# A chunked delta rule: ScalarE's and VectorE's steps put in another order, another bank for an output transpose, and an inversion's 64x64 products paired

## The chip, the cores and the metric

The kernel runs on one core of a Trainium2 chip. The metric is device time in microseconds (us) of one execution: 2244.25 us is the median of three runs before the change (2241.93 to 2248.31). The engines are TensorE (PE; PEld is its weight load), VectorE (DVE), ScalarE (ACT), GpSimd (POOL) and SyncE (SP, which issues most DMAs).

## The reference

A two-layer encoder step over 2048 prompt tokens and 32 sample tokens, width 1024, float32. Layer one is a gated delta rule with 8 heads of 128; layer two is sliding-window attention. What matters here is the delta rule. It is evaluated in blocks of positions; within a block a unit lower triangular matrix has to be inverted (or solved with), and a 128x128 state `s` per head goes from block to block:

```python
lower = jnp.where(strict, jnp.einsum('nbhik,nbhjk->nbhij', kbeta, kc) * decay, 0.0)
tmat = lower + jnp.eye(c, dtype=lower.dtype)
u = lax.linalg.triangular_solve(tmat, vc * bc[..., None], left_side=True, lower=True, unit_diagonal=True)
...
def step(s, xs):
    qd, kd, ui, wi, ai, gl = xs
    v_new = ui - jnp.einsum('bhck,bhkv->bhcv', wi, s)
    o = jnp.einsum('bhck,bhkv->bhcv', qd, s) + jnp.einsum('bhij,bhjv->bhiv', ai, v_new)
    s = s * gl[..., None, None] + jnp.einsum('bhck,bhcv->bhkv', kd, v_new)
    return s, o
```

## The kernel before

The kernel goes through stages: projections of q, k, v with a short convolution (class `P1`, up to about 720 us of the profiled execution), the delta rule with what is left of the gate projection as filler (class `Delta`, about 720 to 1190 us), output products and layer norm (`O1`), the second layer's projections (`P2`) and attention. The change touches only the delta stage.

The delta stage has 17 chunks: one of the 32 sample tokens and 16 of 128 prompt tokens. `Delta.run` is one loop over them, written as generators that are advanced by hand: `go(a, b, ...)` takes one step of each, and the order of these calls is the order in which instructions are put on PE, DVE and ACT (each works its own list in that order). One turn of the loop works on several chunks at once: state products of chunk `ch`, inversion of the next (`nx`), keys, values and triangular matrix of the one after (`n2`), decays of the third (`n3`). The steps by name:

- `lower` (n2): products k k^T into bank `g`, times the decays `E` on DVE into `npr`; ACT copies the diagonal 32x32 blocks to `nb`, DVE transposes them to `L`. `chain` inverts these blocks column by column, 25 columns on POOL, the last six on DVE a turn later. `spread` (two DVE transposes to `tcp`, two ACT writes to `u32`) lays the result out.
- `invert` (nx): builds the 128x128 inverse `u` from 32x32 to 64x64 to 128x128 blocks with products on PE and copies on ACT (`y1`, `ta`, `u`). 64 of the 128 partitions hold the upper half of a head's matrix, 64 the lower half (`halves`).
- `turn_k`, `turn_v` (n2): transposes of k and v on PE, evicted with a scale into `kd` (ACT) and `vn` (first half DVE, second half ACT).
- `decays` (n3): one DVE add into `E`, then eight exponentials on ACT, one a head. `powers` (n2): exponentials of `gb` in place; `fade`: k and q times `gb` on DVE.
- `changes` (ch): products `vp` with `u`, copied to `vs` by ACT; `seen`: output `o`; `advance`: products `sp`, new state on DVE; `squares`, `norms`, `scale`: the norm of `o`; `errors` (nx): `ks` from the new state, `vn` minus `ks`; `emit` (last chunk): `o` transposed into `otr`, times the gate `z`, to memory.

`fill` puts products of the gate projection (`late_z`: bank `ps`, three products for each slice of 128) between the steps as long as there are any (to loop index 11); later ones put output products of `O1` there. The gate's weights come as `w_raw` and are split into `w_hi` (ACT) and `w_lo` (DVE) where `side(False)` stands. PSUM pools of the stage: `pa` (two banks, tag "tr"), `pb` (one bank, used by the inversion), `pc` (two banks, tag "sc": `ks`, `vp`, `sp`, `otr`), `pd` (one, `op`).

Of the kernel before, what the change touches and what calls it, by code (L numbers as in the profile page):

```python
# [95 lines left out]
class P1:  # L96
# [164 lines left out]
                a += w  # L261

    def split(self):
        if self.fetched is not None:
            self.next = split_fetched(self.nc, self.wp, self.fetched, self.sub)
            self.fetched = None

    def late_raw(self, pool, h):

# [180 lines left out]
class Delta:  # L450
# [141 lines left out]
    def turn_v(self, ch):  # L592
        nc, G, n = self.nc, self.G, ch.n
        ch.vn = []
        for q in range(2):
            vn = self.four.tile([128, 4, 128], F32, tag="vn", name="vn")
            tr = self.pa.tile([128, 4, 128], F32, tag="tr", name="vtr")
            for j in range(4):
                nc.tensor.transpose(tr[:n, j, :], ch.v[q][:, j, :n], G["ident"][:, :])
            if q == 0:  # L600
                nc.vector.tensor_tensor(out=vn[:n], in0=tr[:n], in1=self.bc(G["hn"][:n, ch.ti, 0:4], n), op=ALU.mult)
            else:
                for j in range(4):
                    nc.scalar.activation(vn[:n, j, :], tr[:n, j, :], AF.Copy, scale=G["hn"][:n, ch.ti, 4 + j:5 + j])
            ch.vn.append(vn)
            yield

# [45 lines left out]
    def invert(self, ch):  # L653

        nc, V = self.nc, self.nc.vector
        if ch.n == 32:
            return
        u, sml = self.u, self.sml
        u32, npr = self.u32, ch.npr
        halves = (slice(0, 64), slice(64, 128))  # L660

        def new(pool):
            return pool.tile([128, 8, 64], F32, tag="tr", name="bps")

        y1, y1p = self.y1, new(self.pb)
        for p in range(8):
            for r in (0, 64):
                s, t = slice(r, r + 32), slice(r + 32, r + 64)
                nc.tensor.matmul(y1p[t, p, 0:32], npr[s, p, t], ch.tcf[s, p, :], start=True, stop=True)
        for r in (slice(32, 64), slice(96, 128)):  # L670
            nc.scalar.mul(y1[r, :, 0:32], y1p[r, :, 0:32], -1.0)
        yield
        tp = new(self.pa)
        for p in range(8):
            nc.tensor.matmul(tp[:64, p, :], u32[:64, p, :], y1[:64, p, :], start=True, stop=True)
        ta = sml.tile([128, 8, 64], F32, tag="ta", name="ta")
        nc.scalar.copy(ta[:64], tp[:64])
        yield
        up = new(self.pb)
        for p in range(8):  # L680
            for hv in halves:
                nc.tensor.matmul(up[hv, p, :], y1[hv, p, :], u32[hv, p, :], start=True, stop=True)
        nc.scalar.copy(u[0:64, :, 0:64], up[0:64])
        nc.scalar.copy(u[64:128, :, 64:128], up[64:128])
        yield
        y2p = new(self.pa)
        for p in range(8):
            nc.tensor.matmul(y2p[64:128, p, :], npr[:64, p, 64:128], ta[:64, p, :], start=True, stop=True)
        nc.scalar.copy(ta[64:128], y2p[64:128])
        yield  # L690
        u2p = new(self.pb)
        for p in range(8):
            nc.tensor.matmul(u2p[:64, p, :], ta[64:128, p, :], u[64:128, p, 64:128], start=True, stop=True)
        nc.scalar.mul(u[:64, :, 64:128], u2p[:64], -1.0)
        yield

    def errors(self, ch):
# [81 lines left out]
    def emit(self, ch):  # L779

        nc, V, T, n = self.nc, self.nc.vector, self.T, ch.n
        for q in range(2):
            z = ch.z[q]
            tr = self.pc.tile([128, 4, 128], F32, tag="sc", name="otr")
            for j in range(4):
                nc.tensor.transpose(tr[:, j, :n], ch.o[:n, q * 4 + j, :], self.G["ident"][:n, :n])
            V.tensor_tensor(out=z[:, :, :n], in0=tr[:, :, :n], in1=z[:, :, :n], op=ALU.mult)
# [3 lines left out]
    def run(self, chunks, S, first, second, side, done):  # L791
# [7 lines left out]
        def go(*gens):  # L799
            for g in gens:  # L800
                next(g, None)
# [34 lines left out]
        for i in range(len(chunks) + 1):  # L836
# [30 lines left out]
                side(None)  # L867
                side(True)
            go(a, t, a, t, seen, sq)
            side(False)  # L870
            fill(2 * more + gate)
            if i + 4 == len(chunks):
                next(second.gen)
# [8 lines left out]
            if i == 0:  # L882
# [714 lines left out]
def program(tc, I, O, T, G):  # L1597
# [32 lines left out]
    def side(o):  # L1630
        if o is None:
            left.close()
            o1.append(O1(tc, left, I, O, T, G))
        elif o1 and o:
# [4 lines left out]
        elif not o1 and not o:  # L1639
            p1.split()  # L1640

    def outputs():
        tiles = [(t * 128, t * 128, min(128, NT - t * 128)) for t in range(NTT)]
# [206 lines left out]
```

## Time and profile before

| | |
|---|---|
| runs | 2241.93, 2244.25, 2248.31 us |
| profiled execution | 2235.55 us; span from first to last instruction 2233.8 us |
| PE busy | 2161.8 us (97% of the span) |
| DVE, ACT, POOL busy | 1378.5, 900.5, 838.1 us |
| granted PE clock, mean | 0.990 |
| delta stage, 764.31 to 1008.19 us (nine turns) | PE 231.22 busy of 243.88 |

Rows of the profile read as: start, length, engine, line, operation, out<-in, partitions x elements, count; in brackets the engine's idle time just before the row and what ended it. A matmul in float32 leaves two records. Groups give count, busy time and mean length; a window row gives the busy time of each engine in a stretch, the granted clock, DMA share and GB/s. Line numbers are those of the kernel before.

### The profile page before, as it was taken

Reading aid. Unit: us, or ns where it says so; the run is one execution under the profiler, and the core shown is the slowest. Engines: PE = TensorE matmul, PEld = TensorE weight load, DVE = VectorE, ACT = ScalarE, POOL = GpSimd, SP = SyncE. Lnnn points to the kernel's source line nnn. Section 1 sums busy time; section 2 is a strip of 40 time slices with the busy share of each in tenths; the row PEclk is TensorE's granted clock in tenths of the full one; section 3 lists DMA queues with packets and bytes.
Section 4 is the critical chain, followed back from the end, with each engine's and each line's share of the span. In section 5 each row is a group of like instructions: output and inputs, shape, how many; then the busy total and the mean of one; then the engine's idle time right before and its main releaser. Section 6 shows DMA issues by size and latency. Waiting matters only on the chain.

```text
span 2233.8 us, 36601 instructions
## 1 busy us (share of the span) xinstructions
PE 2161.8 (97%) x13706; PEld 1982.5 (89%) x13706; DVE 1378.5 (62%) x2713; ACT 900.5 (40%) x2235; POOL 838.1 (38%) x1189
## 2 busy tenths in 40 slices
PE   8999999999999999999989999999999999999997
PEld 6999999999999888898878788999999977778885
DVE  3676666753476687878867886135442235668774
ACT  4344444433333566667742212222112235445541
POOL 1422122221211477777731201046441214556563
PEclk9999999999999999999999999999999999999999
DMA  5222122333445244345526764365222277233311
GB/s 195 67 64 82 60 75 66 111 104 110 125 121 162 93 132 126 122 127 188 189 103 202 224 200 141 111 219 175 73 75 69 84 178 249 76 95 96 111 59 57
DMA packets 250529, 274.47 MB, mean 123 GB/s; under 512 B 76096, under 2 KB 195200, under 8 KB 250080
## 3 DMA queue, kind: packets, MB, share of 16 engines
q1 hardware_dynamic: 238352, 248.84, 36.3%
q10 hardware_dynamic: 12000, 23.30, 3.0%
q8 instruction: 108, 1.77, 0.3%
q14 instruction: 69, 0.57, 0.1%
HBM read 168.53 MB, written 103.92 MB: 122 GB/s over the span
## 4 chain that ended last, share of the span: by engine, by line
PE 83%; ACT 7%; DVE 4%; DMA 3%; POOL 1%; issue 1%; ACTq 0%; DVEq 0%; SPq 0%; POOLq 0%
PE ps L77 16%; PE ps L79 16%; PE ps L78 16%; PE po L1076 5%; PE po L1078 4%; PE po L1077 4%; PE ot L1567 4%; PE S L1546 2%; PE tr L1561 2%; PE vp L714 1%; DMA act_raw<-s_hT 1%; ACT kd L588 1%; PE op L732 1%; PE sp L744 1%; PE gq L618 1%
## 5 line engine op out<-in xcount | busy, mean ns | idle before, releaser
L77 PE MATMUL ps<-act_hi,w_hi 128*128 128x416 f32 x2000 | 707.0, 354 | 6.4 <-ACT w_hi L53 5.1
L79 PE MATMUL ps<-act_hi,w_lo 128*128 128x416 f32 x2000 | 704.9, 353 | 1.8 <-POOL w_lo L54 1.2
L78 PE MATMUL ps<-act_lo,w_hi 128*128 128x416 f32 x2000 | 701.6, 351 | 0.5 <-DVE act_lo L69 0.4
L77 PEld LDWEIGHTS ps<-act_hi,w_hi 128*128 128x128 f32 x2000 | 376.8, 189 | 11.9 <-ACT w_hi L53 6.1
L79 PEld LDWEIGHTS ps<-act_hi,w_lo 128*128 128x128 f32 x2000 | 376.1, 188 | 6.7 <-POOL w_lo L54 1.7
L78 PEld LDWEIGHTS ps<-act_lo,w_hi 128*128 128x128 f32 x2000 | 376.4, 188 | 5.4 <-DVE act_lo L69 1.1
L54 POOL TENSOR_TENSOR w_lo<-w_raw,w_hi 128x1024 fp32r<-128x1024 f32 x51 | 135.4, 2655 | 555.7 <-ACT w_hi L53 501.5
L196 DVE SCALAR_TENSOR_TENSOR y<-R,convw,y 128x2083 f32<-128x2083 f32 x72 | 173.7, 2414 | 109.7 <-ACT y L194 74.1
L572 POOL TENSOR_TENSOR tm<-L,Tt 128x60 f32<-128x60 f32 (+19 forms) x373 | 141.1, 378 | 119.6 <-DVE tm L572 47.5
L1554 POOL TENSOR_TENSOR P<-P,sm 128x384 f32<-128x384 f32 (+2 forms) x128 | 100.5, 807 | 181.7 <-DVE sm L1433 106.6
L575 POOL TENSOR_TENSOR Tt<-Tt,tm 128x60 f32<-128x60 f32 (+19 forms) x373 | 152.9, 410 | 29.2
L1429 ACT ACTIVATE P<-S,nm 128x192 f32<-128x192 f32 (+2 forms) x260 | 104.6, 418 | 93.3 <-DVE nm L1422 40.4
L227 ACT COPY R<-ps 128x416 f32<-128x416 f32 (+1 forms) x144 | 61.3, 449 | 199.0 <-PE ps L79 174.7
L53 ACT CAST w_hi<-w_raw 128x1024 fp32r<-128x1024 f32 x62 | 64.9, 1047 | 128.8 <-PE ps L78 99.4
L1076 PE MATMUL po<-wo_hi,g_hi 128*128 128x512 f32 x256 | 103.8, 406 | 1.8 <-ACT hT L1183 1.8
L1273 POOL TENSOR_TENSOR rs<-rs,sin 128x416 f32<-128x416 f32 x50 | 71.1, 1421 | 78.8 <-DVE rs L1272 72.1
L1078 PE MATMUL po<-wo_hi,g_lo 128*128 128x512 f32 x256 | 100.6, 393 | 0.0
L1567 PE MATMUL ot<-pt,vd 128*128 128x256 f32 x372 | 98.7, 392 | 1.9 <-ACT pt L1563 1.5
L1077 PE MATMUL po<-wo_lo,g_hi 128*128 128x512 f32 x256 | 100.3, 392 | 0.0
L1076 PE MATMUL po<-wo,g_hi 128*128 128x512 f32 x240 | 99.3, 414 | 0.0
L1078 PE MATMUL po<-wo,g_lo 128*128 128x512 f32 x240 | 96.2, 401 | 0.0
L1077 PE MATMUL po<-wo,g_hi 128*128 128x512 f32 x240 | 96.1, 400 | 0.0
(304 smaller groups left out, 3984.3 us busy)
## 6 DMA issues: line engine op xcount, KB each, us to landing
w_raw<-in_w_in SPq DMA_DIRECT2D x40, 512.0 KB
w_raw<-in_b_w_in SPq DMA_DIRECT2D x20, 512.0 KB
gb<-s_gcum SPq DMA_DIRECT2D x17, 512.0 KB
k<-s_k SPq DMA_DIRECT2D x17, 512.0 KB
s_bz<-za SPq DMA_DIRECT2D x40, 208.0 KB
s_bq<-ra SPq DMA_DIRECT2D x40, 208.0 KB
s_q<-y SPq DMA_DIRECT2D x8, 1024.0 KB
s_k<-y SPq DMA_DIRECT2D x8, 1024.0 KB
```

Of the source, the lines that this page charges most:

```text
L54: sub.tensor_tensor(out=lo[:], in0=raw[:], in1=hi[:], op=ALU.subtract)
L77: nc.tensor.matmul(ps, hi[:, k, :], xh[:, k, :], start=(k == 0), stop=False)
L78: nc.tensor.matmul(ps, hi[:, k, :], xl[:, k, :], start=False, stop=False)
L79: nc.tensor.matmul(ps, lo[:, k, :], xh[:, k, :], start=False, stop=(k == KC - 1))
L196: nc.vector.scalar_tensor_tensor(out=y[:], in0=R[:, j:j + W], scalar=self.convw[:, i, j:j + 1], in1=y[:], op0=ALU.mult, op1=ALU.add)
L572: P.tensor_tensor(out=tm[:n, i0 - k:, :w], in0=L[:n, i0:, j:j + 1].to_broadcast(sh), in1=Tt[:n, j:j + 1, :w].to_broadcast(sh), op=ALU.mult)
L575: P.tensor_tensor(out=Tt[:n, i0:, :w], in0=Tt[:n, i0:, :w], in1=tm[:n, i0 - k:, :w], op=ALU.subtract)
L1076: nc.tensor.matmul(ps[:n], ghi[:, k, :n], w[0][:, k, cs], start=a, stop=False)
L1077: nc.tensor.matmul(ps[:n], ghi[:, k, :n], w[1][:, k, cs], start=False, stop=False)
L1078: nc.tensor.matmul(ps[:n], glo[:, k, :n], w[0][:, k, cs], start=False, stop=z)
L1429: nc.scalar.activation(P[u], src, AF.Exp, bias=nm[:, u:u + 1], scale=1.0, accum_out=sm[:, u:u + 1])
L1567: nc.tensor.matmul(ot[:, p], self.vd[:, kc0 + j, p, :], pt[:, 2 * j:2 * j + 2, :], start=(j == 0), stop=(j == nj - 1))
```

## The change

Five edits, all in the delta stage:

1. `invert` has one step less. The product `tp` of the upper halves and the product that gives the lower half's 64x64 inverse go into one bank, product by product in turn; then the upper half's inverse and the second factor of the off-diagonal block do the same.
2. `turn_v` evicts both halves on ACT, and its first step stands earlier, ahead of `spread` (the layout of the inverted blocks).
3. `powers` moves from the middle of `invert`'s ACT steps to the end of `squares`; the eight exponentials of `decays` move behind the inversion's last copy.
4. The split of a gate weight becomes `cast` (ACT, at the old place) and `subtract` (DVE, at the end of the turn's calls).
5. The first `otr` of a chunk takes the inversion's bank (`pb`) instead of one of `pc`.

```diff
     def split(self):
-        if self.fetched is not None:
-            self.next = split_fetched(self.nc, self.wp, self.fetched, self.sub)
-            self.fetched = None
+        self.cast()
+        self.subtract()
+
+    def subtract(self):
+        if isinstance(self.fetched, tuple):
+            raw, hi, lo = self.fetched
+            self.sub.tensor_tensor(out=lo[:], in0=raw[:], in1=hi[:], op=ALU.subtract)
+            self.next, self.fetched = (hi, lo), None
+
+    def cast(self):
+        raw = self.fetched
+        if raw is not None and not isinstance(raw, tuple):
...
+            self.nc.scalar.copy(hi[:], raw[:])
+            self.fetched = raw, hi, lo
@@ turn_v
-            if q == 0:
-                nc.vector.tensor_tensor(out=vn[:n], in0=tr[:n], in1=self.bc(G["hn"][:n, ch.ti, 0:4], n), op=ALU.mult)
-            else:
-                for j in range(4):
-                    nc.scalar.activation(vn[:n, j, :], tr[:n, j, :], AF.Copy, scale=G["hn"][:n, ch.ti, 4 + j:5 + j])
+            for j in range(4):
+                h = q * 4 + j
+                nc.scalar.activation(vn[:n, j, :], tr[:n, j, :], AF.Copy, scale=G["hn"][:n, ch.ti, h:h + 1])
@@ invert
+        lo, hi = halves
         tp = new(self.pa)
         for p in range(8):
-            nc.tensor.matmul(tp[:64, p, :], u32[:64, p, :], y1[:64, p, :], start=True, stop=True)
+            nc.tensor.matmul(tp[lo, p, :], u32[lo, p, :], y1[lo, p, :], start=True, stop=True)
+            nc.tensor.matmul(tp[hi, p, :], y1[hi, p, :], u32[hi, p, :], start=True, stop=True)
         ta = sml.tile([128, 8, 64], F32, tag="ta", name="ta")
-        nc.scalar.copy(ta[:64], tp[:64])
+        nc.scalar.copy(ta[lo], tp[lo])
+        nc.scalar.copy(u[hi, :, 64:128], tp[hi])
         yield
-        up = new(self.pb)
+        yp = new(self.pb)
         for p in range(8):
-            for hv in halves:
-                nc.tensor.matmul(up[hv, p, :], y1[hv, p, :], u32[hv, p, :], start=True, stop=True)
-        nc.scalar.copy(u[0:64, :, 0:64], up[0:64])
-        nc.scalar.copy(u[64:128, :, 64:128], up[64:128])
-        yield
-        y2p = new(self.pa)
-        for p in range(8):
-            nc.tensor.matmul(y2p[64:128, p, :], npr[:64, p, 64:128], ta[:64, p, :], start=True, stop=True)
-        nc.scalar.copy(ta[64:128], y2p[64:128])
+            nc.tensor.matmul(yp[lo, p, :], y1[lo, p, :], u32[lo, p, :], start=True, stop=True)
+            nc.tensor.matmul(yp[hi, p, :], npr[lo, p, 64:128], ta[lo, p, :], start=True, stop=True)
+        nc.scalar.copy(ta[hi], yp[hi])
+        nc.scalar.copy(u[lo, :, 0:64], yp[lo])
         yield
@@ emit
-            tr = self.pc.tile([128, 4, 128], F32, tag="sc", name="otr")
+            tr = (self.pb.tile([128, 4, 128], F32, tag="tr", name="otr") if q == 0 else
+                  self.pc.tile([128, 4, 128], F32, tag="sc", name="otr"))
@@ run
             go(a, t, a, t, seen, sq)
-            side(False)
+            go(gen(self.powers, n2))
+            side(0)
...
-            go(e, t, t)
+            go(e, t, t, w)
             drain(t)
             if nx:
                 self.spread(nx)
-            go(w, e)
+            go(e)
...
-            p = gen(self.powers, n2)
             go(v)
             fill(gate)
-            go(r, r, r, g, r, r, v, r, k, r, d)
+            go(r, g, r, r, r, r, v, r, k, r, d)
...
-            go(v, r, v)
+            go(v, r)
...
-            go(w, r, p, r, seen, k, r, d, r)
+            go(w, r, r, seen, k, r, r)
...
-            go(v, o, d)
+            go(v, o, d, d)
+            side(1)
```

How the lists move. First ACT, from the copy of `tp` (`ta`) to the two copies `vs` of the products with the inverse, in a steady turn before (`bps` is the inversion's bank, `tr` and `vtr` the transposes of k and v):

```order
L677 COPY ta<-bps 64x512
L588 ACTIVATE kd<-tr,t_ekd 128x128 x4
L683 COPY u<-bps 64x8x64
L684 COPY u<-bps 64x8x64
L689 COPY ta<-bps 64x512
L604 ACTIVATE vn<-vtr,t_hn 128x128 x4
L627 ACTIVATE gb<-gb 128x512 x2
L588 ACTIVATE kd<-tr,t_ekd 128x128 x4
L534 ACTIVATE E<-E,t_ngc 128x128 x4
L694 ACTIVATE u<-bps 64x8x64
L534 ACTIVATE E<-E,t_ngc 128x128 x4
L716 COPY vs<-vp 128x512 x2
```

The same stretch of ACT in the changed kernel:

```order
L690 COPY ta<-bps 64x512
L691 COPY u<-bps 64x8x64
L601 ACTIVATE kd<-tr,t_ekd 128x128 x4
L697 COPY ta<-bps 64x512
L698 COPY u<-bps 64x8x64
L615 ACTIVATE vn<-vtr,t_hn 128x128 x4
L601 ACTIVATE kd<-tr,t_ekd 128x128 x4
L703 ACTIVATE u<-bps 64x8x64
L547 ACTIVATE E<-E,t_ngc 128x128 x8
L725 COPY vs<-vp 128x512 x2
```

`gb` has left the stretch, and all eight `E` stand between the last `u` and `vs`. `gb` and the other half of `vn` now stand at the end of the turn:

```order
L769 ACTIVATE vn,Xo<-o 128x128 x4
L638 ACTIVATE gb<-gb 128x512 x2
L615 ACTIVATE vn<-vtr,t_hn 128x128 x4
L662 ACTIVATE u_5380<-tcp,sides 128x8x32 x2
L313 ACTIVATE zth<-ps 128x416
```

There they follow the squares of the output and precede the writes to `u32` (here `u_5380`), which wait for VectorE's transposes. On PE, the inversion's 64x64 products and what lies between them, before:

```order
L675 MATMUL bps<-y_5392,u_5380 64x64 x8
L585 MATMUL tr<-ident,k 128x128 x4
L682 MATMUL bps<-u_5380,y_5392 64x64 x16
L688 MATMUL bps<-ta,npr 64x64 x8
L599 MATMUL vtr<-ident,v 128x128 x4
L728 MATMUL op<-Sp,q 128x128 x4
L585 MATMUL tr<-ident,k 128x128 x4
L693 MATMUL bps<-u,ta 64x64 x8
```

And in the changed kernel, where each left-out stretch holds seven more couples of the two rows above it:

```order
L687 MATMUL bps<-y_5392,u_5380 64x64
L688 MATMUL bps<-u_5380,y_5392 64x64
...
L598 MATMUL tr<-ident,k 128x128 x4
L695 MATMUL bps<-u_5380,y_5392 64x64
L696 MATMUL bps<-ta,npr 64x64
...
L612 MATMUL vtr<-ident,v 128x128 x4
```

The step L696 reads `ta`, the copy of the first couple's upper half, and the only work between the two is one set of transposes. On DVE, before, the split of a weight stands in the end of the column chain (`tm`, `Tt`), ahead of the transposes to `tcp`:

```order
L54 TENSOR_TENSOR w_lo<-w_raw,w_hi 128x1024
L704 TENSOR_TENSOR vn<-vn,ks 128x512
L575 TENSOR_TENSOR Tt<-Tt,tm 128x4x7
L572 TENSOR_TENSOR tm<-L,Tt 128x24
L575 TENSOR_TENSOR Tt<-Tt,tm 128x24
```

In the changed kernel it stands after the scaling of the output by its norm:

```order
L785 TENSOR_TENSOR o<-o,ro_y 128x1024
L270 TENSOR_TENSOR w_lo<-w_raw,w_hi 128x1024
L646 TENSOR_TENSOR k<-k,gb 128x1024
L563 TENSOR_TENSOR npr<-g,E 128x512
L646 TENSOR_TENSOR q<-q,gb 128x512
```

So it moves from the end of one turn's list to the middle of the next.

More of the change, by code (lines that the diff above doesn't have):

```diff
@@ L263, in split @@
     def split(self):
-        if self.fetched is not None:
-            self.next = split_fetched(self.nc, self.wp, self.fetched, self.sub)
-            self.fetched = None
+        self.cast()
[8 more added lines that the diff above has]
+        if raw is not None and not isinstance(raw, tuple):
+            hi = self.wp.tile([128, KC, 128], F32R, tag="w_hi", name="w_hi")
+            lo = self.wp.tile([128, KC, 128], F32R, tag="w_lo", name="w_lo")
+            self.nc.scalar.copy(hi[:], raw[:])
+            self.fetched = raw, hi, lo
     def late_raw(self, pool, h):
@@ L692, in invert @@
         for p in range(8):
-            nc.tensor.matmul(u2p[:64, p, :], ta[64:128, p, :], u[64:128, p, 64:128], start=True, stop=True)
-        nc.scalar.mul(u[:64, :, 64:128], u2p[:64], -1.0)
+            nc.tensor.matmul(u2p[lo, p, :], ta[hi, p, :], u[hi, p, 64:128], start=True, stop=True)
+        nc.scalar.mul(u[lo, :, 64:128], u2p[lo], -1.0)
         yield
@@ L1633, in side @@
             o1.append(O1(tc, left, I, O, T, G))
-        elif o1 and o:
+        elif o1 and o is True:
             next(o1[0].on.rest, None)
@@ L1638, in side @@
             o1[0].steps += 1
-        elif not o1 and not o:
+        elif not o1 and o is False:
             p1.split()
+        elif not o1 and o == 0:
+            p1.cast()
+        elif not o1 and o == 1:
+            p1.subtract()
     def outputs():
```

## The prediction, made before the changed kernel ran

> **What bounds the kernel now.** I read the windows first, cut at the start of the `vp` products (L714), which run once in each turn of the chunk loop. The columns are length, then busy time of each engine, granted clock, DMA share, GB/s.
>
> ```profile
> 764.31:1008.19 243.88, 231.22 (x2441) 215.97 (x2441) 193.66 (x462) 166.18 (x518) 174.30 (x442) 1.00 0.40 126
> 791.59:818.14 26.55, 25.71 (x272) 24.07 (x272) 21.14 (x52) 18.03 (x58) 19.22 (x50) 1.00 0.40 128
> 818.14:846.10 27.96, 25.88 (x272) 24.08 (x272) 22.39 (x53) 19.01 (x59) 20.53 (x51) 1.00 0.44 140
> 1033.64:1057.51 23.87, 21.61 (x249) 19.80 (x249) 19.70 (x50) 17.63 (x57) 18.42 (x47) 1.00 0.71 234
> ```
>
> The first row holds nine turns, 27.1 us each. They come in two kinds: 26.55, and 27.96 where a gate weight is split. PE is busy 25.8 of them, so it bounds this stretch, with about 1.3 us a turn lost in waits. In the later turns (last row) the gate products no longer fill PE: 21.6 busy of 23.87.
>
> Next I read the timeline of PE through one turn, from the first 64x64 product of the inversion to the `vp` products, and of ScalarE (ACT) beside it.
>
> ```profile
> 863.25 1.14 PE L675 MATMUL bps<-y,u 64*64 64x64 f32 x16
> 864.32 0.66 PE L585 MATMUL tr<-ident,k 128*128 128x128 f32 x4
> 864.91 0.97 PE L682 MATMUL bps<-u,y 64*64 64x64 f32 x26
> ...
> 866.74 0.66 PE L599 MATMUL vtr<-ident,v 128*128 128x128 f32 x4
> ...
> 868.66 1.14 PE L693 MATMUL bps<-u,ta 64*64 64x64 f32 x16
> 869.73 1.16 PE L549 MATMUL g<-k 128*128 128x128 f32 x8
> 871.04 1.16 PE L549 MATMUL g<-k 128*128 128x128 f32 x8 [0.15 <-ACT kd L588]
> 872.65 2.05 PE L714 MATMUL vp<-vn,u 128*128 128x128 f32 x16 [0.45 <-ACT u L694]
> 874.54 0.60 PE L786 MATMUL otr<-ident,o 128*128 128x128 f32 x4
> 875.38 0.66 PE L786 MATMUL otr<-ident,o 128*128 128x128 f32 x4 [0.24 <-ACT vs L716]
> ```
>
> ```profile
> 864.49 0.58 ACT L677 COPY ta<-bps 64x512 f32<-64x512 f32 x1 [2.56 <-PE bps L675]
> 865.02 1.14 ACT L588 ACTIVATE kd<-tr,t_ekd 128x128 f32<-128x128 f32 x4
> 866.10 0.58 ACT L683 COPY u<-bps 64x512 f32<-64x512 f32 x1
> 866.69 0.58 ACT L684 COPY u<-bps 64x512 f32<-64x512 f32 x1
> 867.18 0.58 ACT L689 COPY ta<-bps 64x512 f32<-64x512 f32 x1
> 867.78 1.14 ACT L604 ACTIVATE vn<-vtr,t_hn 128x128 f32<-128x128 f32 x4
> 868.80 1.17 ACT L627 ACTIVATE gb<-gb 128x512 f32<-128x512 f32 x2
> 869.84 1.15 ACT L588 ACTIVATE kd<-tr,t_ekd 128x128 f32<-128x128 f32 x4
> 870.84 1.31 ACT L534 ACTIVATE E<-E,t_ngc 128x128 f32<-128x128 f32 x4
> 872.00 0.60 ACT L694 ACTIVATE u<-bps 64x512 f32<-64x512 f32 x1
> ...
> 873.85 0.58 ACT L716 COPY vs<-vp 128x512 f32<-128x512 f32 x1
> ...
> 875.23 1.64 ACT L554 COPY nb<-npr 32x256 f32<-32x256 f32 x4
> ```
>
> From 865.02 ACT runs without a gap until 872.60, and `vp` starts 0.05 us after `u` (L694) is done. So in this part of each turn ACT's queue sets the time: the last 64x64 product ended by 869.8, and its copy lay behind the exponentials of `gb`, four scalings for `kd` and four exponentials of `E`, until 872.00.
>
> **The change part by part.** *The pairing.* The groups of the nine turns (name, count, busy us, mean ns):
>
> ```profile
> L682 PE MATMUL bps<-u,y 64*64 64x64 f32 x288 | 10.3, 221 | 0.0
> L675 PE MATMUL bps<-y,u 64*64 64x64 f32 x144 | 10.3, 221 | 0.0
> ```
>
> Each product leaves two records. Sixteen products on two alternating corners of the array (L682) cost 10.3/9 = 1.14 us a turn, the same as eight on one corner (L675). The old steps occupy PE from 863.25 to 864.32 (1.07), 864.91 to 866.74 (1.83, two steps that overlap at the seam) and 868.66 to 869.73 (1.07): 3.97 us. The new ones are pair, pair, single. The first new pair stands on the same two corners as L682, so 1.07. The second is a kind that the trace does not show: both halves read partitions 0 to 63 and write different column halves. It lies between 1.07 (as L682) and 2.14 (no overlap, 16 times L675's cost of one). I take 1.07, since L682 too alternates corners with every product at no cost; 2.14 stays in the range. Sum 3.21, so 0.76 us of PE less.
>
> Here the Trainium skill has two pages that disagree. "TensorEngine Tiling (Array Packing)", Key Properties, says that different tiles execute weight loads and matmuls in parallel, which would make the pair 1.07. "TensorE: Matmul & The Clock Gate", Part 3, The mechanism, says that a weight load overlaps running matmuls only when the row group differs; the new pair shares its row group, and by that rule it would be 2.14 or more. No row here decides between them.
>
> *ACT's order.* I walk the same turn with the new order, keeping 863.25. PE: pair to 864.32, `tr` to 864.91. ACT: `ta` 864.49, upper `u` 865.02 to 865.60, then `kd` (1.08 to its successor) to 866.68. The second pair needs `ta`, done 865.07; with 0.1 for the hand-over it starts at 865.17, so PE loses 0.26 that it did not lose before, when independent products stood there. It ends 866.24. `ta` upper at 866.68, `u` lower 867.2 to 867.8, `vn` to about 868.8, `kd` to 869.85. PE goes on with `vtr` at 866.24 and needs 1.92 us (866.74 to 868.66) to the last product: 868.16, after `u` lower. That ends 869.23. ACT takes its copy at 869.85, right behind `kd`, since `gb` (1.04) and `E` have left this place: done 870.45. PE: `g` at 869.23, `g` at 870.1, `vp` at 871.0, with `u` ready 0.55 earlier. `vp` moves from 872.65 to 871.0: 1.65 us, of which 0.76 is products and the rest waits.
>
> *What the eight exponentials now delay.* They run from 870.35 in one piece; four take 872.00 - 870.84 = 1.16, so eight 2.3, to 872.7. `vs` then starts 1.7 us after `vp` instead of 1.2. The first `otr` waited for a bank that `vs` frees; in its new bank it does not. It starts 1.89 after `vp` as now (872.9); the second needs the first `vs` (873.3) and starts near 873.4, 2.4 after `vp` instead of 2.73. So the delay of `vs` is covered by the bank, and about 0.3 is gained more. The turn becomes 26.55 - 1.65 - 0.3 = 24.6 us. If that cover failed, the 0.5 would come back.
>
> *VectorE's side.* In every second turn the split of a weight stands in VectorE's chain ahead of the transposes on which the inversion waits:
>
> ```profile
> 883.41 1.23 DVE L54 TENSOR_TENSOR w_lo<-w_raw,w_hi 128x1024 fp32r<-128x1024 f32 x1 [1.57 <-ACT w_hi L53]
> ...
> 886.80 0.68 DVE L645 STREAM_TRANSPOSE tcp<-Tt 128x256 f32<-128x256 f32 x1
> ```
> ```profile
> 887.53 0.69 PE L669 MATMUL bps<-tcp,npr 32*32 32x32 f32 x32 [0.50 <-DVE tcp L645]
> ```
>
> That is 2.8 us of VectorE, and the reason for 27.96 against 26.55. The change puts the cast and the subtraction apart, the latter behind the scaling of `o`, where VectorE has time. So both kinds of turn become the 24.6 kind. In the turn without a split:
>
> ```profile
> 858.28 0.70 DVE L645 STREAM_TRANSPOSE tcp<-Tt 128x256 f32<-128x256 f32 x1
> 859.02 0.45 DVE L646 STREAM_TRANSPOSE tcp<-tcp 128x256 f32<-128x256 f32 x1
> ```
> ```profile
> 860.41 0.69 PE L669 MATMUL bps<-tcp,npr 32*32 32x32 f32 x32
> ```
>
> VectorE is 0.94 ahead of PE. Its chain is released by `nb`, which by the walk moves from 875.23 to 873.85, 1.38 earlier, while PE comes 1.95 earlier: 0.37 remains, so no new wait, but little. The moved `vn` (1.14, L604's price, on ACT where VectorE had it) and `gb` (1.04), with the cast, stand in ACT's gap before the next `u32`; that gap was 4.61 us in the turn with a cast, longer than 2.2, so they cost nothing.
>
> ```profile
> 887.99 0.91 ACT L651 ACTIVATE u<-tcp,sides 128x256 f32<-128x256 f32 x2 [4.61 <-DVE tcp L646]
> ```
>
> The weight's DMA goes later past `z`, `v` and `q` on SP's queue; its buffer is needed a turn or more later, so nothing.
>
> *What is late next.* GpSimd (POOL) runs the inversion's first 25 columns as one chain per turn; its first row shows its idle time:
>
> ```profile
> 879.44 0.26 POOL L572 TENSOR_TENSOR tm<-L,Tt 128x31 f32<-128x31 f32 x1 [3.49 <-DVE tm L572]
> ...
> 907.36 0.26 POOL L572 TENSOR_TENSOR tm<-L,Tt 128x31 f32<-128x31 f32 x1 [3.91 <-DVE tm L572]
> ...
> 1064.31 0.26 POOL L572 TENSOR_TENSOR tm<-L,Tt 128x31 f32<-128x31 f32 x1 [0.46 <-DVE tm L572]
> ```
>
> The chain takes 907.36 - 879.44 - 3.91 = 24.0 us in a turn with a split, and about 23.87 - 0.46 = 23.4 in a late turn. The change does nothing to it. 24.6 stays above it, so PE still bounds the nine turns; the late turns can only fall to some 23.6.
>
> *The sum.* Nine turns: 243.88 - 9 x 24.6 = 22.5. The turn before them, which has no inversion in its steady place, 1. The turn after them, still partly filled, I put at 1.5, an estimate below the 2.5 of the nine; the two late turns 0.3 each, from 23.87 to POOL's 23.6; the last chunks, where output products fill PE, 0 to 1.6, I take 0.4. Together 26 us. The profiled execution, 2235.55 us (span 2233.8 and 1.75 around it), would be 2209.5. It lies 8.7 under the median of the three runs, 2244.25, and I take the 26 off the median: 2218.
>
> **The rivals.** (a) *The second pair does not overlap.* 1.07 us more each turn: 25.67, the nine turns save 12.9, the late ones the same as POOL allows: 14 in all, 2230. For it: the two halves use the same partitions, and no row shows that overlapping. Against it: L682's weight loads and products pass two at a time without any loss.
>
> (b) *The clock drops.* In the late turns PE idles more, and in one of them the clock fell:
>
> ```profile
> 1081.53:1108.85 27.32, 24.37 (x248) 22.40 (x249) 21.57 (x51) 18.76 (x58) 22.77 (x58) 0.88 0.53 175
> ...
> 1098.00:1100.00 2.00, 2.00 (x15) 1.55 (x15) 1.90 (x6) 0.58 (x1) 1.76 (x4) 0.50 0.00 0
> ```
>
> The granted clock was 0.50 inside this turn, which took 27.32 us, 3.4 more than the 23.87 of its neighbour; over the nine filled turns it was 1.00. With 0.76 us less work in turns that POOL holds at 23.6, PE is idle 2.8 instead of 2.3 in each. Four such drops more are 13 to 14, leaving a gain of about 13: 2231. The Trainium skill, "TensorE: Matmul & The Clock Gate", Part 1, has the clock halve after a window of about 3.4 us without activity; the row agrees that it halves.
>
> (c) *Slower: the two column halves take turns.* If alternating within one row group lets each record finish before the next starts, the pair costs 32 times the mean of 221 ns, 7.1 us instead of 1.07. The turn becomes 30.6, 3.5 more than now, 32 us over the nine, and about 4 in each of five later ones: 51 slower, 2295. It decides from 1.07 + 2.5 = 3.6 us, or 112 ns a record. Against it: no pair in the trace behaves so.
>
> (d) *It does more:* the existing drop of the clock goes too (3.4) and the last chunks gain their 1.6 and more: 32 to 36 saved, 2210.
>
> **How the numbers follow.** Forecast 0.52, (a) 0.25, (b) or another new wait of that size 0.10, (c) 0.05, (d) 0.08. The range reaches from (d) to beyond (a) and (b), where half of VectorE's 0.37 is lost as well: 2208 to 2236. 0.3%, about what a measurement here can tell from no change, is 6.7 us; a tenth of (a) and half of (b) might end within it. Faster 0.87, same 0.07, slower 0.06.
>
> **What would show it.** Right: `vp` starts 24.4 to 24.9 us apart between the first and tenth, both kinds alike; no wait of `vp` for `u`; the second pair's 32 records busy 1.1 us; POOL idle about 1 us or less before each chain. Wrong: the second pair at 2 us or more; a wait of the 32x32 products for `tcp` in most turns (VectorE the bound); more stretches at clock 0.50.

## The result, and the profile after

The changed kernel takes 2210.99 us, median of four runs (2206.11 to 2212.92); beside it the kernel before took 2243.36 us (2241.93 to 2248.31). The ratio is 0.9849, 95% interval 0.9826 to 0.9871: 32.4 us less. Forecast were 2218 us, 26 less, in a range of 2208 to 2236; the size that came is that of the prediction's rival (d), 2210 us and 32 to 36 less. The profiled execution took 2210.41 us, span 2208.6, which is 25.1 less than that of before.

The windows of the profile after, cut at the start of the `vp` products (now L723); the first row holds nine turns, the next two are single ones with and without a weight's split:

```profile
760.38:981.58 221.20, 220.86 (x2443) 209.95 (x2441) 191.31 (x452) 174.35 (x555) 176.96 (x442) 1.00 0.45 139
809.43:834.02 24.59, 24.59 (x274) 23.40 (x273) 21.88 (x51) 19.98 (x64) 19.67 (x49) 1.00 0.48 139
834.02:858.62 24.60, 24.60 (x275) 23.41 (x273) 21.08 (x51) 18.89 (x63) 20.49 (x53) 1.00 0.50 160
```

Before, the nine turns took 243.88 with PE busy 231.22. Now PE is busy 220.86 of 221.20. Of the 22.7 us, 10.4 are busy time of PE and 12.3 are its idle time, of which 0.3 is left. Of the 10.4 only some 3 are less work; the rest went with the waits, as e1 below shows. The two kinds of turn are alike.

The timeline of PE through one turn after:

```profile
850.74 0.27 PE L687 MATMUL bps<-y,u 64*64 64x64 f32 x1
...
851.82 0.66 PE L598 MATMUL tr<-ident,k 128*128 128x128 f32 x4
852.41 0.32 PE L695 MATMUL bps<-u,y 64*64 64x64 f32 x2
852.62 0.27 PE L696 MATMUL bps<-ta,npr 64*64 64x64 f32 x1
...
852.73 0.22 PE L696 MATMUL bps<-ta,npr 64*64 64x64 f32 x1
852.74 0.22 PE L695 MATMUL bps<-u,y 64*64 64x64 f32 x1
852.79 0.22 PE L696 MATMUL bps<-ta,npr 64*64 64x64 f32 x1
...
853.70 0.66 PE L612 MATMUL vtr<-ident,v 128*128 128x128 f32 x4
...
855.61 1.14 PE L702 MATMUL bps<-u,ta 64*64 64x64 f32 x16
856.68 2.10 PE L562 MATMUL g<-k 128*128 128x128 f32 x16
858.62 1.95 PE L723 MATMUL vp<-vn,u 128*128 128x128 f32 x16
860.41 1.17 PE L796 MATMUL otr<-ident,o 128*128 128x128 f32 x8
861.41 1.06 PE L741 MATMUL op<-vs,at 128*128 128x128 f32 x8
```

No row has a wait in brackets. One wait is too short for a bracket: the first product of L696 starts 0.21 behind that of L695 and 0.05 after `ta` (L690, below) is done. From the first 64x64 product to `vp` it is 858.62 - 850.74 = 7.88 us, where it was 872.65 - 863.25 = 9.40. And ACT beside it:

```profile
851.99 0.58 ACT L690 COPY ta<-bps 64x512 f32<-64x512 f32 x1 [2.58 <-PE bps L688]
...
854.37 0.58 ACT L697 COPY ta<-bps 64x512 f32<-64x512 f32 x1
854.96 0.58 ACT L698 COPY u<-bps 64x512 f32<-64x512 f32 x1
855.44 1.12 ACT L615 ACTIVATE vn<-vtr,t_hn 128x128 f32<-128x128 f32 x4
856.45 1.12 ACT L601 ACTIVATE kd<-tr,t_ekd 128x128 f32<-128x128 f32 x4
857.45 0.61 ACT L703 ACTIVATE u<-bps 64x512 f32<-64x512 f32 x1
857.92 2.47 ACT L547 ACTIVATE E<-E,t_ngc 128x128 f32<-128x128 f32 x8
860.26 1.08 ACT L725 COPY vs<-vp 128x512 f32<-128x512 f32 x2
```

The last `u` is done at 858.06, 0.56 ahead of `vp`; the exponentials stand behind it.

### The profile page after: what moved, and what is told of

Read it like the earlier page. It is cut to its first block, busy times and chain, and to the rows that moved or that the text cites. A ratio compares the mean times of both kernels' runs of the same rounds, so it can differ in the third digit from the quotient of the medians.

```text
span 2208.6 us, 36656 instructions
## 1 busy us (share of the span) xinstructions
PE 2144.0 (97%) x13706; PEld 1972.4 (89%) x13706; DVE 1375.8 (62%) x2696; ACT 916.0 (41%) x2303; POOL 841.6 (38%) x1189
## 3 DMA queue, kind: packets, MB, share of 16 engines
q8 instruction: 108, 1.77, 0.3%
## 4 chain that ended last, share of the span: by engine, by line
PE 85%; DMA 4%; POOL 3%; DVE 3%; ACT 3%; issue 1%; ACTq 0%; SPq 0%; DVEq 0%; POOLq 0%
PE ps L77 17%; PE ps L79 17%; PE ps L78 17%; PE po L1087 4%; PE po L1089 4%; PE po L1088 4%; PE ot L1578 4%; PE S L1557 2%; PE tr L1572 2%; POOL Tt L588 1%; POOL tm L585 1%; DMA act_raw<-s_hT 1%; PE g L562 1%; PE op L737 1%; PE op L741 1%
## 5 line engine op out<-in xcount | busy, mean ns | idle before, releaser
L54 POOL TENSOR_TENSOR w_lo<-w_raw,w_hi 128x1024 fp32r<-128x1024 f32 x44 | 117.1, 2661 | 473.9 <-ACT w_hi L53 433.1
L588 POOL TENSOR_TENSOR Tt<-Tt,tm 128x60 f32<-128x60 f32 (+19 forms) x373 | 158.4, 425 | 29.2
L53 ACT CAST w_hi<-w_raw 128x1024 fp32r<-128x1024 f32 x48 | 50.3, 1049 | 116.2 <-PE ps L78 92.3
```

The source lines that it names most:

```text
L54: sub.tensor_tensor(out=lo[:], in0=raw[:], in1=hi[:], op=ALU.subtract)
L588: P.tensor_tensor(out=Tt[:n, i0:, :w], in0=Tt[:n, i0:, :w], in1=tm[:n, i0 - k:, :w], op=ALU.subtract)
```

## The experiments

Total times of one kernel differ by some microseconds between runs: the changed kernel, run again beside the last experiments, gave a ratio of 0.9869 (0.9853 to 0.9884) to the kernel before. Turn lengths repeat far better: its nine turns took 221.35 us there and 221.20 here. So most edits are judged by turns. "Late" is the stretch of four turns from the eleventh to the fifteenth start of the 32x32 products; in it the granted clock stood at 0.50 for 6.8 us in the runs before, e5, e8, e9 and c1, for 3.4 us in e2 and c3, and at 1.00 throughout in the others.

| kernel | nine turns | one turn | late | ratio to before (95%) |
|---|---|---|---|---|
| before | 243.88 | 26.55 and 27.96 | 99.65 | 1 |
| changed | 221.20 | 24.60 | 94.23 | 0.9849 (0.9826-0.9871) |
| changed again | 221.35 | 24.6 | 94.47 | 0.9869 (0.9853-0.9884) |
| old steps (e1) | 224.42 | 24.95 | 95.17 | 0.986 (0.9833-0.9888) |
| before, pairs only (e2) | 242.27 | 26.7 and 27.3 | 98.61 | 0.9991 (0.9973-1.0008) |
| halves 8 and 8 (e3) | 224.42 | 24.95 | 94.83 | 0.985 (0.9822-0.9878) |
| split back (e4) | 228.84 | 24.6 and 26.1 | 94.36 | 0.9886 (0.9864-0.9908) |
| old bank (e5) | 225.16 | 25.08 | 95.39 | 0.9888 (0.9871-0.9905) |
| old exponentials (e6) | 236.58 | 26.27 | 96.18 | 0.9961 (0.9946-0.9976) |
| vn on VectorE (e7) | 221.31 | 24.6 | 94.43 | 0.9872 (0.9854-0.9891) |
| GpSimd one less (e8) | 221.34 | 24.6 | 93.50 | 0.9857 (0.9836-0.9878) |
| mask twice (e9) | 223.38 | 25.1 and 24.6 | 98.28 | 0.9884 (0.9869-0.9899) |
| gates spread (c1) | 219.51 | 23.4 to 25.0 | 95.83 | 0.9863 (0.9846-0.9879) |
| gates and late (c3) | 219.95 | 23.3 to 25.0 | 94.97 | 0.9858 (0.984-0.9876) |

**e1: the new order with the old five steps.** In `invert` the steps `tp`, `up`, `y2p` and `u2p` stand again as the diff's minus lines have them, and the loop takes one more:

```diff
-            go(v, r)
+            go(v, r, v)
```

> The new order of ScalarE and VectorE and the new bank stay; the inversion's 64x64 products go back to their five unpaired steps. Theory (the pairing is worth its 0.76 us of TensorE work a turn and no more, since the queue of ScalarE that held vp is shortened by the reordering): the nine filled turns become 24.6 + 0.7 = 25.3 us, vp still waits for no u, and the whole is about 8 us slower than the changed kernel. Rival (the pairing brings nearly everything, because it brings the copies of u forward): the turns go back to 26.5 or more, 20 to 25 us slower.

Measured: 24.95 a turn, no wait for `u`. Its nine turns:

```profile
762.05:986.47 224.42, 224.02 (x2443) 214.74 (x2442) 191.29 (x452) 174.98 (x554) 174.63 (x440) 1.00 0.45 137
```

PE is busy 3.2 us more than in the changed kernel, 0.35 a turn, and that is the whole of the difference. The rival falls; of the theory, 0.7 was twice too much. Without any pairing the new order saves 243.88 - 224.42 = 19.5 of the 22.7 us. Here PE has the same products as before, and yet it is busy 224.02 instead of 231.22. So 7.2 us of the busy time before were no work: PE stopped 35 times in the nine turns before and once here, and around a stop the records overlap less with their neighbours (the two `g` were two rows of 1.16 before and are one of 2.10 in the timeline above). That is 0.2 us a stop, an estimate from these figures, on top of the idle time that the profile shows.

**e2: the pairs alone.** The kernel before gets `invert` as changed, and nothing else:

```diff
-            go(v, r, v)
+            go(v, r)
```

> The kernel before with the paired products alone, all the rest as before. Theory (ScalarE's queue of exponentials and scalings sets when vp may start): TensorE does 0.76 us less a turn but vp waits for u by as much more; turns stay near 26.5 and 27.9, and the kernel is 0 to 2 us faster than before. Rival (TensorE's work is the bound): each turn is 0.76 us shorter, 9 to 12 us in all.

Measured: 26.7 and 27.3 a turn, the nine turns 1.6 us shorter, the total's interval reaches over 1. Its windows and one turn's PE:

```profile
764.50:1006.77 242.27, 225.56 (x2440) 210.16 (x2440) 193.66 (x462) 166.87 (x518) 175.22 (x442) 1.00 0.40 127
```
```profile
870.30 1.16 PE L549 MATMUL g<-k 128*128 128x128 f32 x8 [0.81 <-ACT kd L588]
871.95 2.05 PE L712 MATMUL vp<-vn,u 128*128 128x128 f32 x16 [0.49 <-ACT u L692]
```

PE is busy 5.7 us less over the nine turns and idles 4.1 of it away: `vp` still waits 0.49 for `u`, and the second `g` waits 0.81 for `kd` where it waited 0.15. Less work on an engine that waits for another's queue turned into more waiting. The theory holds, except that the turns with a split became 0.6 shorter and the others 0.15 longer.

**e3: the second couple as eight and eight.**

```diff
         for p in range(8):
             nc.tensor.matmul(yp[lo, p, :], y1[lo, p, :], u32[lo, p, :], start=True, stop=True)
+        for p in range(8):
             nc.tensor.matmul(yp[hi, p, :], npr[lo, p, 64:128], ta[lo, p, :], start=True, stop=True)
```

> The changed kernel with one thing altered: in the second couple the eight products of one column half are issued first and then the eight of the other, where they alternate now. Theory (two corners that share their rows run side by side only while consecutive products alternate between them, at 29 ns a record): the couple takes 2.1 us, about 1.07 more, turns 25.6, the whole about 11 us slower. Rival (TensorE overlaps weight loads and products whatever the order, or the couple's length is hidden): turns stay 24.6, 0 to 2 us.

Measured: 24.95, between the two. One turn's PE:

```profile
850.84 0.97 PE L695 MATMUL bps<-u,y 64*64 64x64 f32 x13
...
852.67 0.66 PE L612 MATMUL vtr<-ident,v 128*128 128x128 f32 x4
```

The couple occupies PE for 1.83 us, where the alternating one took 853.70 - 852.41 = 1.29, with 0.21 of waiting for `ta` in it. So alternation does what the theory says, but the two halves overlap at their seam, and the first half covers the wait for `ta`: 0.54 instead of 1.07. Of that, 0.19 is given back in the changed kernel behind the couple: `g` to `vp` takes 1.94 there and 1.88 here, `otr` to `op` 1.00 and 0.87. What remains is 0.35, the same as in e1.

**e4: cast and subtraction of the weight both at the old place.**

```diff
-            side(0)
+            side(False)
```

> The changed kernel with cast and subtraction of a gate weight both back at their old place, ahead of the transposes on which the inversion waits. Theory (2.8 us of VectorE there against a lead of 0.4): in every second filled turn the 32x32 products wait for tcp by 1.9 to 2.5 us; those turns 26.5 to 27, the others 24.6; 10 to 14 us slower in all. Rival (VectorE catches up unseen): turns 24.6, no difference.

Measured: turns with a split 26.1 to 26.2, the others 24.6. The first turn with a split took 27.5; in it the granted clock stood at 0.50 from 777.9 to 781.3 us. VectorE's row of the split, and PE's of the wait:

```profile
825.38 1.23 DVE L270 TENSOR_TENSOR w_lo<-w_raw,w_hi 128x1024 fp32r<-128x1024 f32 x1 [2.40 <-ACT w_hi L278]
```
```profile
829.39 0.69 PE L680 MATMUL bps<-tcp,npr 32*32 32x32 f32 x32 [1.43 <-DVE tcp L656]
```

The mechanism is the theory's, its price 1.5 us a split instead of 1.9 to 2.5: VectorE stood further ahead of PE than the 0.4 assumed. Over the nine turns the run is 7.6 us longer; four splits at 1.5 are 6 of them, and the rest lies in the first turn, where the clock fell.

**e5: the first output transpose in its old bank.**

```diff
-            tr = (self.pb.tile([128, 4, 128], F32, tag="tr", name="otr") if q == 0 else
-                  self.pc.tile([128, 4, 128], F32, tag="sc", name="otr"))
+            tr = self.pc.tile([128, 4, 128], F32, tag="sc", name="otr")
```

> The changed kernel with the first output transpose back in the bank that it had, which ScalarE's copy vs must free. Theory (the eight exponentials delay vs by 0.5 us and only the new bank covers that): otr starts 0.5 us later, filled turns 25.1 instead of 24.6, some 5 us in all. Rival (the transposes have room anyway): 24.6, no difference.

Measured 25.08 a turn, and the wait at its place:

```profile
862.26 1.14 PE L795 MATMUL otr<-ident,o 128*128 128x128 f32 x8 [0.34 <-ACT vs L725]
```

`otr` starts 2.29 after `vp` (859.97) instead of 1.79. The theory holds to 0.02 us a turn.

**e6: the exponentials back ahead of `u`.**

```diff
-            go(gen(self.powers, n2))
             side(0)
@@
             d = gen(self.decays, n3)
+            p = gen(self.powers, n2)
@@
-            go(w, r, r, seen, k, r, r)
+            go(w, r, p, r, seen, k, r, d, r)
@@
-            go(v, o, d, d)
+            go(v, o, d)
```

> The changed kernel with the exponentials of gb and the second half of E back in ScalarE's queue ahead of the last copy u; pairs, bank, vn and the split of the weight stay as changed. Theory (the 2.2 us of exponentials ahead of u are what held vp; u is ready 0.5 ahead in the changed kernel): vp waits for u again, filled turns 25.8 to 26.2, some 11 to 14 us slower than the changed kernel. Rival (the pairs bring u early enough): 24.6 to 24.8.

Measured 26.27 a turn, 15.4 us over the nine turns. One turn's PE:

```profile
866.49 1.16 PE L562 MATMUL g<-k 128*128 128x128 f32 x8 [0.83 <-ACT kd L601]
868.14 2.05 PE L723 MATMUL vp<-vn,u 128*128 128x128 f32 x16 [0.49 <-ACT u L703]
```

It is the first half of `E`, not the second, that stands ahead of `u` again. Both waits of the kernel before are back, though pairs, bank and split are new. A little over the theory's 26.2, since `gb` delays `kd` too. Among the parts undone alone this is by far the largest: of a gain of 1.3 to 1.5% over the kernel before, 0.4% is left.

**e7: the first half of `vn` back on VectorE, at its new place.**

```diff
+            if q == 0:
+                nc.vector.tensor_tensor(out=vn[:n], in0=tr[:n], in1=self.bc(G["hn"][:n, ch.ti, 0:4], n), op=ALU.mult)
+            else:
+                for j in range(4):
+                    nc.scalar.activation(vn[:n, j, :], tr[:n, j, :], AF.Copy, scale=G["hn"][:n, ch.ti, 4 + j:5 + j])
```

> The changed kernel with the first scaling of v back on VectorE, at its new early place. Theory (it stood in a gap of ScalarE of over 2 us, and VectorE has no more than 0.4 to spare in the late turns): filled turns 24.6 to 24.8, late turns up to 0.4 longer, 0 to 3 us slower in all. Rival (ScalarE has become too full): the turns become shorter than 24.6.

Measured: 24.6, late turns as in the changed kernel (94.43 against 94.23). This edit costs and brings nothing; the 0.4 a late turn that the theory feared did not come, since VectorE waits for GpSimd there (0.52 and 1.31 us in two of these turns).

**e8 and e9: GpSimd in the late turns.** Two late turns after, cut at the 32x32 products, and the wait that ends one of them:

```profile
1017.36:1040.53 23.17, 20.80 (x248) 19.34 (x248) 19.45 (x49) 19.42 (x61) 19.26 (x50) 1.00 0.60 198
1040.53:1064.53 24.00, 20.81 (x248) 19.34 (x248) 20.67 (x50) 19.54 (x61) 20.08 (x50) 1.00 0.63 212
```
```profile
1017.36 0.69 PE L680 MATMUL bps<-tcp,npr 32*32 32x32 f32 x32 [1.15 <-DVE tcp L656]
```

GpSimd has no gap between 994 and 1112 us. The longer turn has one operation of VectorE more, the subtraction for an output weight, and GpSimd is 0.82 busier for the same work. Rows of VectorE and of GpSimd there:

```profile
1044.22 1.38 DVE L542 TENSOR_TENSOR E<-gb,nm 128x1024 f32<-128x1024 f32 x1
1045.52 1.32 DVE L1061 TENSOR_TENSOR wo_lo<-wo_raw,wo_hi 128x1024 fp32r<-128x1024 f32 x1
```
```profile
1044.60 1.17 POOL L585 TENSOR_TENSOR tm<-L,Tt 128x72 f32<-128x72 f32 x1
1045.84 1.20 POOL L588 TENSOR_TENSOR Tt<-Tt,tm 128x72 f32<-128x72 f32 x1
1047.12 0.32 POOL L585 TENSOR_TENSOR tm<-L,Tt 128x68 f32<-128x68 f32 x1
```

A step of GpSimd that takes 0.32 takes 1.2 when a long operation of VectorE with both operands in SBUF runs beside it. e8 shortens GpSimd's chain, e9 adds such an operation.

```diff
+    for c in chunks[12:]:
+        c.split = 24
```

> The changed kernel with the chain of GpSimd one column shorter (24 of 31 instead of 25) in the last chunks, VectorE doing one more. Theory (GpSimd without a gap sets the 23.1 to 24.0 us of the late turns): each becomes 0.3 to 0.7 us shorter, 1 to 2 us in all. Rival (VectorE sets them): each 0.4 us longer, 2 us slower in all.

```diff
-        V.tensor_tensor(out=ch.E[:n, :, :n], in0=ch.gb[:n, :, :n], ...)
+        for _ in range(2):
+            V.tensor_tensor(out=ch.E[:n, :, :n], in0=ch.gb[:n, :, :n], ...)
```

> The changed kernel with VectorE's addition of the mask to E (128x1024, both operands in SBUF, 1.22 to 1.38 us) issued twice, at a place where VectorE later waits for ScalarE anyway; the result is the same. Theory (a VectorE operation with both operands in SBUF holds up GpSimd for its length, so GpSimd's chain grows by 0.9 to 1.2 us a turn, and GpSimd had 0.6 us a turn to spare in the filled turns and nothing in the late ones): filled turns 24.9 to 25.2 in the mean, late ones 0.9 to 1.2 longer, 7 to 11 us slower in all. Rival (GpSimd is not touched, and VectorE with 4 us idle a turn takes it in): 24.6, no difference.

e8: the late stretch is 93.50 against 94.23 and 94.47, 0.2 a turn less, under the theory's 0.3 to 0.7. The clock fell in two of its four turns; the two at 1.00 took 22.86 and 24.12, where the changed kernel has 23.05 and 24.00. In the first of these GpSimd now waits for VectorE, and the 32x32 products that end it wait longer:

```profile
1011.52 0.26 POOL L585 TENSOR_TENSOR tm<-L,Tt 128x31 f32<-128x31 f32 x1 [0.40 <-DVE tm L585]
```
```profile
1017.59 0.69 PE L680 MATMUL bps<-tcp,npr 32*32 32x32 f32 x32 [1.56 <-DVE tcp L656]
```

So VectorE stands right behind GpSimd in the shorter kind of turn, and one column less buys almost nothing. Why it buys nothing in the longer kind, where VectorE still waits for GpSimd, stays open. e9, the late stretch, and the doubled operation with GpSimd beside it:

```profile
997.89:1096.17 98.28, 86.23 (x993) 80.44 (x993) 85.92 (x201) 77.72 (x244) 82.56 (x201) 0.97 0.59 205
```
```profile
1049.55 2.64 DVE L543 TENSOR_TENSOR E<-gb,nm 128x1024 f32<-128x1024 f32 x2
```
```profile
1049.92 1.17 POOL L586 TENSOR_TENSOR tm<-L,Tt 128x72 f32<-128x72 f32 x1
1052.46 1.16 POOL L586 TENSOR_TENSOR tm<-L,Tt 128x68 f32<-128x68 f32 x1
```

One more step of GpSimd takes 1.2, and the late turns are 0.95 longer each in the mean (98.28 against 94.47 in the changed kernel beside it). The first two, with the clock at 1.00 in both kernels, are 0.85 and 0.77 longer; the other two, in which the clock fell, 1.05 and 1.14. So the direction is the theory's, and the price about 0.8, just under its 0.9 to 1.2. GpSimd still has no gap there, and VectorE waits for it longer than before (1.67 against 0.84 in the second of these turns), so it is GpSimd's chain that grew. The filled turns became 24.8 in the mean (223.38 / 9), just under its range, and the nine take 2.0 us more; there PE also waits for ScalarE's `o` in some, so GpSimd alone is not shown as the cause. The total is 3.6 us over the changed kernel, less than the 7 to 11 expected.

**c1 and c3: can it be better?** The filled turns are now PE's work and nothing else, the late ones leave PE idle for 2 to 3 us. So the gate products were spread over one turn more (c1), and the late turns eased with e8's column and an earlier half of the exponentials (c3).

```diff
-    OPEN = 11
+    OPEN = 12
@@
-            more, gate = 0.0 if n2 else 1.0, 1.13 if i < self.OPEN else 0.0
+            more, gate = 0.0 if n2 else 1.0, 1.04 if i < self.OPEN else 0.0
@@
-            if i == 14:
+            if i in (13, 14):
```

> The changed kernel with the gate products spread over twelve turns instead of eleven (1.04 where 1.13 stood, OPEN 12), and the loads of the output weights that follow made up one turn later. Theory (TensorE's work alone sets the filled turns, and the late turns have 2 to 3 us of TensorE idle that GpSimd covers): filled turns 24.2 in the mean, the twelfth 24.5, 2 to 3 us faster than the changed kernel. Rival (GpSimd's chain, 24.0 in the mean, is already as close): turns stay over 24.5 and nothing is gained.

```diff
+    for c in chunks[12:]:
+        c.split = 24
@@
-            go(v, o, d, d)
+            go(*((d, v, o, d) if i > self.OPEN else (v, o, d, d)))
```

> The last one with two more edits for the late turns alone: GpSimd's chain one column shorter (24), and the first half of E's exponentials ahead of the last copy u, so that VectorE does not wait for them. Theory (in the late turns GpSimd and, right behind it, VectorE's wait for E set the time): late turns 23.0 to 23.4 instead of 23.1 to 24.0, 4 to 6 us faster than the changed kernel in all. Rival (u delays vp and gives it back): late turns as before, 2 to 3 us.

Neither beats the changed kernel: 2208.24 and 2207.32 us beside 2208.85, with overlapping intervals. The nine turns of c1 take 1.8 us less, but the gate products come in steps that can't be divided, so only three of the nine turns lost one (18 products instead of 24; 23.4 to 24.0 us) and the others came out at 24.6 to 25.0, and the late stretch, with the clock at 0.50 for 6.8 us, is 1.4 longer. In c3, 1.4 of the nine turns is gained and 0.5 lost late, with the clock at 0.50 for 3.4 us. Both expectations, 2 to 3 and 4 to 6 us faster, were missed.

> The changed kernel once more, beside the others on the same chip: 2207 to 2213 us, filled turns 24.6.

It gave 2208.85 us and 24.6 a turn.

## Why the prediction was right, point by point

**ACT's queue as the limit: shown.** e6 brings the wait of `vp` for `u` back and 15.4 us with it, e2 keeps the queue and gains 1.6 only, and e1 has 19.5 of the 22.7 without any pairing. One reading of the prediction was too low: it had about 1.3 us a turn lost in waits. The idle time is 12.66 / 9 = 1.4, and by e1 some 0.8 more a turn lay hidden in PE's busy time. The walk through the turn met the trace closely. Counted from the first 64x64 product, the second pair's end was forecast at 2.99 us and came at 2.96, the last product at 4.91 and 4.87, `vp` at 7.75 and 7.88. (The copy that the walk calls upper `u` is the lower half's inverse; the order is as it says.) The 0.13 lies in `g`, which takes 1.94 to `vp` where the walk had 1.77. It takes 1.88 in e3, so the walk's price was 0.11 too low; the other 0.06 is likely a wait of the second `g` for `kd`, too short for the profile to show.

**The pairing: direction right, size too kind to it.** The second pair overlaps. Its groups over the nine turns:

```profile
L695 PE MATMUL bps<-u,y 64*64 64x64 f32 x144 | 11.2, 224 | 0.0
L696 PE MATMUL bps<-ta,npr 64*64 64x64 f32 x144 | 10.3, 221 | 0.0
```

They are 1.24 and 1.14 us a turn and lie on top of each other: in the timeline above the next record of L696 comes 0.06 us after the last, with one of L695 between them. Rivals (a) and (c) fall. "TensorEngine Tiling (Array Packing)" of the Trainium skill, Key Properties, has different tiles work in parallel, and the row agrees; the rule of the Trainium skill's "TensorE: Matmul & The Clock Gate", Part 3, The mechanism, by which the pair would have been 2.14, does not describe it. But the 0.76 us of products were worth 0.35 a turn: 0.21 went to the wait for `ta`, which the forecast had (0.26), and 0.19 to slower rows behind it (e3).

**The bank and the split: shown.** The bank's cover, which the walk priced at 0.5, is worth 0.48 in e5. The split's 2.8 us of VectorE are worth 1.5 in e4, and both kinds of turn are alike, as forecast. Taken back alone, exponentials, split, bank and pairing cost 15.4, 7.6 (6 without the fall of the clock), 4.0 and 3.2 us over the nine turns. That is 29 to 30 and not 22.7; I take it that one part's wait hides another's, which no run shows by itself.

**VectorE's and ACT's reserves: held.** There is no wait of the 32x32 products for `tcp` in the nine turns. GpSimd's gap was forecast at 1 us or less and is 1.21 in every second turn:

```profile
865.19 0.26 POOL L585 TENSOR_TENSOR tm<-L,Tt 128x31 f32<-128x31 f32 x1 [1.21 <-DVE tm L585]
```

**Terms that were mis-sized.** The nine turns gave 22.7 (forecast 22.5). "The turn before: 1" was 3.9 by the start of the first `vp` (764.31 to 760.38): 1.5 is the same walk in that turn, and 2.4 is that the first 32x32 products came earlier, at 749.66 instead of 752.06. More than half of the 2.4 goes with the clock. Between 715 us and these products it stood at 0.50 for 10.2 us before and for 6.8 us here. Seven of the other profiles with the new order also have 10.2 us, and these products at 750.75 to 751.41; the two with the old order have them at 752.06 and 752.08. So about 1 us came with the new order. "The turn after: 1.5" was 2.4 (25.45 to 23.06), since all of the reordering works there, too. From there to the output transposes, where 1.0 was forecast for late turns and last chunks, 3.1 came. Here, too, the clock plays in: it stood at 0.50 for 13.7 us of this part before and for 10.2 us here, and the profile of the changed kernel run again, with 13.7 us, gained 2.1. In all, those transposes start 32.1 us earlier, not 26:

```profile
L1181 PE MATMUL tr<-ident,r x8: 270/272/273, 1181.3 to 1183.5; 128*128 128x128 f32 x8
```
```profile
L1192 PE MATMUL tr<-ident,r x8: 270/272/273, 1149.2 to 1151.4; 128*128 128x128 f32 x8
```

In the changed kernel run again, whose clock fell for as long as before in both places, they start at 1151.73, 29.6 earlier; that is the better measure of the change. The medians differ by 32.4 here and by 30.6 beside the last experiments. So the forecast of 26 was some 4 us too small, in its terms for the stretches around the nine turns, and the other 2.5 of the profiled 32.1 go with the clock, which is luck. In the profiled pair 6.9 are lost behind this point (1052.5 us to the end before, 1059.4 after). The change doesn't touch that part, and in the profiles of the twelve experiments, which all have the same code there, it took 1048.4 to 1059.6 us; so I take the 6.9 for scatter between runs, which is argued from these numbers and not tested.

**The clock.** Rival (b) did not come. The late turns have PE idle for 2.4 to 3.2 us each and stand at 1.00. Rival (d)'s saving came, but not the end of the clock's falls that it went by: behind the nine turns the clock fell at 1096.7 and 1154.7 us before, and it still falls twice, now both times in the turn that starts at 1099.03, among the last chunks:

```profile
1099.00:1103.00 4.00, 3.97 (x21) 3.98 (x22) 3.06 (x3) 2.02 (x3) 3.61 (x6) 0.57 0.29 64
1123.00:1130.00 7.00, 6.72 (x46) 5.93 (x47) 3.28 (x14) 1.97 (x4) 0.00 (x0) 0.53 0.20 74
```

Each fall that ends before the program does lasts 3.41 us or a multiple of it in all these profiles (6.83, 10.24, 17.07). What sets where it falls was not tried.

## What to carry to other kernels

An engine that is 97% busy can still be held by another engine's queue: look which row ends just ahead of the one that waits, and what stands ahead of that row in its own queue. Removing work from the waiting engine then brings next to nothing (1.6 us in e2), moving two steps out of the way of the awaited one brings most of the gain (e6), and the cover that the move uses up (here a bank) has to be found in the same edit (e5). Where turns repeat, compare turn lengths of profiled executions: they repeat to 0.03 us where totals scatter by microseconds. Look at the granted clock of the stretch first, since a fall of it shifts single turns by more than some edits are worth.

## What the runs showed of the hardware

A stop of PE cost more than the idle time in the profile: some 0.2 us of busy time went with each (e1, an estimate).

Two 64x64 tiles that use the same rows and different columns of the array ran side by side at 29 ns a record while they alternated; eight products of one tile came at 58 ns a record (13 records from 850.84 to 851.60 in e3).

VectorE's `tensor_tensor` with both operands in SBUF held GpSimd up: steps of 0.32 took 1.2. Beside one that reads a PSUM bank they did not; in the changed kernel:

```profile
1051.25 0.69 DVE L563 TENSOR_TENSOR npr<-g,E 128x512 f32<-128x512 f32 x1 [0.87 <-ACT E L547]
```
```profile
1051.51 0.33 POOL L585 TENSOR_TENSOR tm<-L,Tt 128x70 f32<-128x70 f32 x1
```

"SBUF — State Buffer" of the Trainium skill, Who interferes with whom, says that VectorE with two SBUF inputs and a GpSimd operation that reads SBUF exclude each other; these rows agree. So the length of GpSimd's chain depends on what VectorE does beside it. The late turns come in two lengths, 23.2 and 24.0, where the forecast had one floor of 23.6, and the 0.8 that e9's added operation cost in turns at full clock is the size of that difference.
